# Where weights stand within their places: an offset of a few columns in a transformer layer

## The chip, the core and the metric

The kernel runs on one core of one Trainium2 chip. The metric is the device time of one execution in microseconds; lower is better. The core has a matrix engine (TensorE, in the profile PE, with its weight loads as PEld), a vector engine (VectorE, DVE), an activation engine (ScalarE, ACT), GpSimd (POOL) and SyncE (SP), which issues transfers. SBUF is the on-chip memory of 128 partitions from which the engines read; PSUM takes the results of matmuls, here in banks of 512 fp32 columns.

## What is computed

One transformer layer on a sequence of 512 tokens with 1024 features, in fp32:

```python
h = modulate(rmsnorm(x, norm_ffn1), sh1, sc1)
x = x + 0.5 * g1 * swiglu(h, w_ffn1_in, w_ffn1_out)
h = modulate(rmsnorm(x, norm_mix), sh2, sc2)
qa, ka, va, qb, kb, vb, ga, gb = split(h @ w_in)
ya = window_gqa_sink(rope(qa), rope(ka), va, sink) @ w_branch_a
ob = rmsnorm(diff_attention(rope(qb), rope(kb), vb, lam), subln_b) * (1 - lam_init)
yb = ob @ w_branch_b
x = x + g2 * ((sigmoid(ga) * ya + sigmoid(gb) * yb) @ w_out)
h = modulate(rmsnorm(x, norm_ffn2), sh3, sc3)
x = x + 0.5 * g3 * swiglu(h, w_ffn2_in, w_ffn2_out)
```

The feed-forward width is 2816, `shift`, `scale` and gate `g` of each part come from a conditioning vector, and each SwiGLU splits its incoming product into gate and up half.

## The kernel before

Features stand on the 128 partitions and tokens along the columns, so x is eight tiles of 128 x 512. To keep fp32 accuracy every operand of a product is split into a high part of type fp32r and a low part that holds what is left, and a product is three matmuls: high x high, high x low, low x high (`mm3`, lines 168 to 171; `two`, lines 433 to 441, does this for two outputs with a moving operand of 256 columns).

**Weights and their places.** A tile of weights is 128 x 1024 fp32 (512 KB) or, in the outgoing product of the first SwiGLU, 128 x 128 per input chunk. It comes from HBM into one of four `raw` buffers. ScalarE copies it to the high part, VectorE subtracts to get the low part (`split_from`, lines 179 to 181). In `load_main` (line 973) ScalarE writes the negated copy and a transfer of GpSimd's queue adds the weights to it. High and low parts stand in two long tensors, `high` and `low`, of five places of 1024 columns each. `high_low` (line 186) hands the places out in turn, skipping those held by a feed-forward unit:

```python
i = i * 1024 + aside
return tuple(t[:, i : i + n] for t in parts)
```

`aside` is an offset in columns (4 bytes each) within the place. It is 0, `ASIDE` = 16 or `FAR` = 64. The tensors are 16 columns longer than the five places. A full tile with an offset hangs over into the next place by as many columns, and the framework that adds the waits sees this overlap: the tile then also waits for the readers of those columns in the next place. Before the change the offset is

- 0 in the first SwiGLU's first products, in `project` (line 1031: v, k and q of the second attention), in `project_pairs` (line 1048), in `gates` (line 1077) and in `branch` (line 1498);
- 16 in the feed-forward units (`Unit.prepare`, line 477), in the mix (line 1563) and in the last four outgoing tiles of the first SwiGLU;
- 64 in the other outgoing tiles (`Out1.prepare`, line 771; 768 or 512 columns, so nothing hangs over).

Activations stand in tiles of other tensors: h, the attention outputs and the merged branches in `b8` tiles, the transposed probabilities and some sums in `u4` tiles.

**Order of the work around the change.** The first SwiGLU ends with `Out1`. For its last chunk group the outputs m = 4 to 7 are formed by halves of the tokens in `boundary` (line 355), so that the norm of the first half can run while the second is multiplied: all four m for tokens 0 to 255 (matmuls of 256 columns), then all four again for 256 to 511. Then come the first three gates, by halves, with weights in `u4`, and the projections of v, k and q, where h is the stationary operand and the weights of 512 columns move. `main` (line 1513) goes on with gates 3 and 4 (`EARLY_A` = 5 is where they stop), then `project_pairs` for k and v and for q of the window attention: there, too, h is stationary, and 256 columns of weights move, 48 matmuls a tile, six tiles. The differential attention's scores, transposes and products are put between those matmuls by `Line`, which keeps a list of due pieces at build time. The other gates (5 to 15) are filler while attention runs; their weights are loaded by `load_main` as the stationary operand, with 512 columns of h moving.

Then `branch` multiplies the differential attention's output with w_branch_b for all 512 tokens, beside the window attention, and after that the window attention's output with w_branch_a by halves of the tokens: for each half four tiles of weights, 24 matmuls of 256 columns each. The results, times the gate, are summed in `then_b` (line 1538) by VectorE, which frees one of three `acc` banks, and are split for the mix. The mix multiplies with w_out, eight tiles: six for all tokens (24 matmuls of 512 columns each), the last two by halves (`LAST` = 2) for the norm of the second SwiGLU. The second SwiGLU then runs units with offset 16.

TensorE's order is fixed by the program in these stages; ScalarE, VectorE and the queues of SP and POOL are ordered by the framework's scheduler at build time, outside the parts marked as a manual schedule.

Of the kernel before, what the change touches and what calls it, by code (L numbers as in the profile page):

```python
# [18 lines left out]
P = 128  # L19
D = 1024  # L20
T = 512
NC = D // P
# [77 lines left out]
ASIDE = 16  # L100

FAR = 64

CHUNKS = (range(0, 6), range(6, 12), range(12, 16), range(16, 22))
PLAIN, LAST_1 = 3, 4
# [10 lines left out]
EARLY_A, FETCH = 5, 4.0  # L116
# [13 lines left out]
def layer(ctx: ExitStack, tc: tile.TileContext, a: dict):  # L130
# [10 lines left out]
    def sbuf(tag, shape, dt, bufs):  # L141
        return sb.tile(shape, dt, name=name(tag), tag=tag, bufs=bufs)
# [4 lines left out]
    def f2():  # L147
        return sbuf("f2", [P, T], F32, F2)

    def b8(dt=F32R):  # L150
        return sbuf("b8", [P, 4, T], dt, 12)

    def u4(dt=F32R):
        return sbuf("u4", [P, 2, T], dt, 6)
# [24 lines left out]
    def split_from(hi, lo, src):  # L179
        S.copy(hi, src)  # L180
        V.tensor_tensor(lo, src, f(hi), ALU.subtract)  # L181
# [4 lines left out]
    def high_low(n=1024, aside=0, holder=None):  # L186
        while turn[0] % HILO in holders:
            turn[0] += 1
        i = turn[0] % HILO
        turn[0] += 1  # L190
        if holder:
            holders[i] = holder
        i = i * 1024 + aside
        return tuple(t[:, i : i + n] for t in parts)
# [5 lines left out]
    def load_split(src, n=1024, spare=False, aside=0):  # L200
        raw = sbuf("raw", [P, 1024], F32, RAW)
        if spare:
            hi, lo = (u4().rearrange("p a b -> p (a b)") for _ in range(2))
        else:
            hi, lo = high_low(aside=aside)
        nc.sync.dma_start(raw[:, 0:n], src)
        split_from(hi[:, 0:n], lo[:, 0:n], raw[:, 0:n])
        return hi, lo

    HALVES = (slice(0, 2 * P), slice(2 * P, T))  # L210
    FULL = (slice(0, T),)
# [231 lines left out]
    class Unit:  # L443
# [33 lines left out]
        def prepare(self, q):  # L477

            if q in self.ready:
                return  # L480
            self.ask(q)
            n = self.depth * 2 * P
            if q in self.apart:
                both = b8().rearrange("p a b -> p (a b)")
                hi, lo = both[:, 0:n], both[:, 1024 : 1024 + n]
            else:
                hi, lo = high_low(n, ASIDE, (self, q))
            t = self.at[q]
            with tc.issue_after(copied[0]) if q in self.in_order and copied else nullcontext():
                split_from(hi, lo, t)  # L490
            self.ready[q] = hi, lo
            if q in self.more:
                s, src = self.more[q]
                G.dma_start(t, self.srcs[src], accum_op=ALU.add)
                self.at[s] = t
# [105 lines left out]
    with tc.manual_schedule(engines=BOUND | {mybir.EngineType.SP, mybir.EngineType.Pool}):  # L601
# [60 lines left out]
        for k in range(NC):  # L662
# [17 lines left out]
            wh, wl = w1.pop(k)[3:]  # L680
# [72 lines left out]
    class Out1:  # L753
# [17 lines left out]
        def prepare(self, m):  # L771
            if m not in self.ready:
                self.ask(m)
                t = self.ready[m] = high_low(self.depth * P, ASIDE if self.by_halves(m) else FAR, (self, m))
                with tc.issue_after(copied[0]):
                    split_from(*t, self.at[m])

# [51 lines left out]
    with tc.manual_schedule(engines={mybir.EngineType.SP, mybir.EngineType.Pool}):  # L829
# [4 lines left out]
        for q in range(3, 2 * PLAIN):  # L834

            w = loaded1 or [load_split(a["w1i"][q - 3, k], aside=ASIDE * (q == 5)) for k in range(2)]
            loaded1 = None
            out = pair_banks()
            for k in range(NC):
                wh, wl = w[k // 4]  # L840
                for i in range(2):
                    o = (k % 4) * 256 + i * P
# [11 lines left out]
        for n, chunks in enumerate(CHUNKS):  # L854
# [3 lines left out]
            for p in range(begun, max(chunks.stop // 2, PLAIN + 1)):  # L858
                u, nxt = units1[p], units1.get(p + 1)
# [73 lines left out]
    for i in range(2):  # L933
        o = ROW_LAM + 2 * i * HD
# [35 lines left out]

    hh, hl = new_h()

    def load_main(src):

        raw = sbuf("raw", [P, 1024], F32, RAW)
        nc.sync.dma_start(raw, src)
        hi, lo = high_low()
        S.copy(hi, raw)
        S.activation(lo, raw, AF.Identity, scale=-1.0)
        G.dma_start(lo, src, accum_op=ALU.add)  # L980
        return hi, lo
# [66 lines left out]
    def project_pairs(srcs, then):  # L1048

        n = 2 * P  # L1050
        out = [bank("acc") for _ in range(2)]
        for u, src in enumerate(srcs):
            wh, wl = load_main(src)
            for t in range(NT):
                ht = slice(t * P, (t + 1) * P)
                po = out[t // 2][:, t % 2 * n : (t % 2 + 1) * n]
                for i in range(4):
                    k = 4 * u + i
                    w = slice(i * n, (i + 1) * n)
                    first, last = k == 0 and t % 2 == 0, k == NC - 1 and t % 2 == 1  # L1060
                    PE.matmul(po, hh[k][:, ht], wh[:, w], start=first, stop=False, skip_group_check=True)
                    PE.matmul(po, hh[k][:, ht], wl[:, w], start=False, stop=False, skip_group_check=True)
                    PE.matmul(po, hl[k][:, ht], wh[:, w], start=False, stop=last, skip_group_check=True)
                    yield MM3 / 2
        then(out)
# [11 lines left out]
    def gates(more=lambda: True):  # L1077
        while gate_next[0] < 16 and more():
            j = gate_next[0]
            gate_next[0] += 1  # L1080
            wh, wl = load_main(a["w_gate"][j])
            out = bank("acc")
            for k in range(NC):
                o = k * P
                mm3(out, wh[:, o : o + P], wl[:, o : o + P], hh[k], hl[k], k == 0, k == NC - 1)
                yield MM3
            gate_end(j, out)
# [202 lines left out]
    wa = {}  # L1290
# [204 lines left out]
            turns["w"] = (b, g * nk + kc + 1)  # L1495


    def branch(w, j0, o_h, o_l, then, load, r=FULL[0]):
        for u in range(4):
            with tc.issue_after(banded_last[0]):  # L1500
                wh, wl = load(w[u])
            for i in range(2):
                j = 2 * u + i
                g = f2()[:, r]
                nc.sync.dma_start(g, gate_scr[j0 + j][:, r])
                y = bank("acc")[:, r]
                for k in range(4):
                    o = k * 256 + i * P
                    mm3(y, wh[:, o : o + P], wl[:, o : o + P], o_h[:, k, r], o_l[:, k, r], k == 0, k == 3)
                    yield MM3 * (r.stop - r.start) / T  # L1510
                then(j, g, y, r)

    def main():
        yield from beside(project(vb_w, T, values_b), LATER)
        yield from beside(project(a["w_kb"], T, keys_b), LATER)
        yield from beside(project(a["w_qb"], T, queries_b), LATER)
        yield from beside(gates(lambda: gate_next[0] < EARLY_A), 1)
        while later or asked:
            column(later)
        tables_a()  # L1520
        yield from project_pairs([a["w_kva"][u] for u in range(2)], keys_a)
        for g in range(2):
            yield from project_pairs([a["w_qa"][2 * g + u] for u in range(2)], lambda ps, g=g: queries_a(ps, g))
        yield from gates(lambda: done["b"] < NT)
        line.drain(lambda: done["b"] == NT)
        start_a()
        yield from gates()
        ma = [b8(F32) for _ in range(2)]

        def then_a(j, g, y, r):  # L1530
            V.scalar_tensor_tensor(ma[j // 4][:, j % 4, r], g, 1.0, y, ALU.add, ALU.mult)
            line.helped(0.6)

        yield from branch(a["w_yb"], 8, ob_h, ob_l, then_a, load_main)
        mix.extend(new_h())
        mh, ml = mix

        def then_b(j, g, y, r):
            V.scalar_tensor_tensor(g, g, 1.0, y, ALU.add, ALU.mult)
            m = ma[j // 4][:, j % 4, r]  # L1540
            V.tensor_tensor(m, m, g, ALU.add)
            split_from(mh[j][:, r], ml[j][:, r], m)
            line.helped(1.0)

        for i, r in enumerate(HALVES):
            line.drain(lambda: done["a"] >= 2 * i + 2)
            yield from branch(a["w_ya"], 0, *wa["o"], then_b, load_split, r)

    mix = []
    line.run(main())  # L1550
# [9 lines left out]
    nc.sync.dma_start(cact[0], c_scr.partition_broadcast(P))  # L1560
    mod_begin(G3)
    for m in range(NC):
        w = load_split(a["w_mix"][m], aside=ASIDE)

        def products(po, r, w=w):
            wh, wl = w
            for k in range(NC):
                o = k * P
                mm3(po, wh[:, o : o + P], wl[:, o : o + P], mh[k][:, r], ml[k][:, r], k == 0, k == NC - 1)
                yield  # L1570

        if m >= NC - LAST:
            last.append((m, products))
            continue
        y = bank("sc")
        list(products(y, FULL[0]))
        V.scalar_tensor_tensor(x[m], y, modv[G2][:, m : m + 1], x[m], ALU.mult, ALU.add)
        n3.add(m)
        for _ in range(BESIDE_MIX[m]):
            if latest or asked:  # L1580
                column(latest)
# [242 lines left out]
    u = units[2]  # L1824
# [19 lines left out]
    for v, p in seq:  # L1844
# [7 lines left out]
        u = v  # L1852
# [77 lines left out]
```

## Time and profile before

| | |
|---|---|
| time, median of 3 runs | 1067.63 us (1066.71 to 1070.24) |
| profiled execution | 1065.94 us, its span 1064.2 us |
| matmul records | 7316 |
| moved by DMA | 220.92 MB, mean 208 GB/s |

The profile is one execution as the hardware profiler recorded it. Windows give the busy time of each engine in a stretch of the span. Groups gather equal instructions of a line: the number behind x is the count, then total busy time and the mean in ns of one, then the idle time before them. A name such as `sc<-b,high` says that a PSUM bank sc is written from an activation in b and a weight in high. A matmul's record runs from its start to its modelled end, so records of neighbours overlap.

### The profile page before, as it was taken

The numbers are of one execution on the slowest core, as the hardware profiler recorded it, in microseconds if no ns is written. First come the engines' busy times: TensorE is split into PE (matmuls) and PEld (weight loads), VectorE is DVE, ScalarE is ACT, GpSimd is POOL, SyncE is SP. The second block draws the span as 40 slices with busy tenths as digits, with TensorE's granted clock in tenths as the row PEclk, the third lists the DMA queues.
The fourth block names the chain that finished last, engine by engine and source line by source line (L and its number), as shares of the span: only waits on it lengthen the run. The fifth ranks groups of instructions, "written<-read, shape, count | busy, mean of one in ns | idle before, by whom it ended". The sixth has DMA issues, their size and how long they took to land.

```text
span 1064.2 us, 18654 instructions
## 1 busy us (share of the span) xinstructions
PE 1048.2 (99%) x7316; PEld 955.1 (90%) x7316; DVE 795.8 (75%) x1459; ACT 567.3 (53%) x928; POOL 154.0 (14%) x174
## 2 busy tenths in 40 slices
PE   8999999999999999999999999999999999999998
PEld 6789889899998988898778878989999999999998
DVE  7985667567796679858863587976888787877867
ACT  5564335334354432666775756534766646654553
POOL 1100010100110100443211100001111211112210
PEclk8999999999999999999999999999999999999999
DMA  9968686966885369696357843974498998989974
GB/s 342 365 205 198 210 216 186 281 174 191 257 203 173 120 238 410 208 257 164 82 126 182 232 144 100 358 234 109 101 231 191 227 229 216 220 217 220 213 149 124
DMA packets 69083, 220.92 MB, mean 208 GB/s; under 512 B 8193, under 2 KB 10881, under 8 KB 68994
## 3 DMA queue, kind: packets, MB, share of 16 engines
q1 hardware_dynamic: 46512, 146.52, 38.5%
q0 software_dynamic: 19488, 68.70, 34.7%
q10 hardware_dynamic: 2994, 4.51, 1.2%
q8 instruction: 57, 0.93, 0.4%
q14 instruction: 32, 0.26, 0.1%
HBM read 209.46 MB, written 10.23 MB: 206 GB/s over the span
## 4 chain that ended last, share of the span: by engine, by line
PE 81%; DVE 8%; issue 5%; ACT 3%; DMA 2%; POOL 1%; SPq 0%; DVEq 0%; POOLq 0%; ACTq 0%
PE acc L439 6%; PE acc L441 6%; PE acc L440 6%; PE sc L439 5%; PE sc L440 5%; PE sc L441 5%; PE sc L169 5%; PE sc L170 5%; PE sc L171 5%; PE acc L169 4%; PE acc L170 4%; PE acc L171 4%; PE sc L177 2%; PE acc L1042 2%; PE acc L1043 2%
## 5 line engine op out<-in xcount | busy, mean ns | idle before, releaser
L180 ACT CAST high<-raw 128x1024 fp32r<-128x1024 f32 (+2 forms) x162 | 158.3, 986 | 168.3 <-PE sc L170 41.7
L181 DVE TENSOR_TENSOR low<-raw,high 128x1024 fp32r<-128x1024 f32 (+2 forms) x162 | 183.7, 1142 | 50.7 <-ACT high L180 46.2
L439 PE MATMUL acc<-b,high 128*128 128x256 f32 x508 | 141.0, 278 | 0.3 <-DVE f L518 0.3
L440 PE MATMUL acc<-b,high 128*128 128x256 f32 x508 | 140.6, 277 | 0.1
L441 PE MATMUL acc<-b,low 128*128 128x256 f32 x508 | 140.6, 277 | 0.0
L439 PE MATMUL sc<-b,high 128*128 128x256 f32 x500 | 138.5, 277 | 0.0
L441 PE MATMUL sc<-b,low 128*128 128x256 f32 x500 | 138.5, 277 | 0.1
L440 PE MATMUL sc<-b,high 128*128 128x256 f32 x500 | 138.4, 277 | 0.0
L181 DVE TENSOR_TENSOR low<-u,high 128x1024 fp32r<-128x1024 f32 (+1 forms) x73 | 87.5, 1200 | 30.4 <-ACT high L180 28.9
L180 ACT CAST high<-u 128x1024 fp32r<-128x1024 f32 (+1 forms) x73 | 75.5, 1036 | 58.4 <-PE sc L170 16.9
L169 PE MATMUL sc<-b,high 128*128 128x512 f32 (+1 forms) x280 | 101.0, 361 | 0.0
L170 PE MATMUL sc<-b,high 128*128 128x512 f32 (+1 forms) x280 | 100.7, 360 | 0.0
L171 PE MATMUL sc<-b,low 128*128 128x512 f32 (+1 forms) x280 | 100.6, 359 | 0.0
L439 PEld LDWEIGHTS acc<-b,high 128*128 128x128 f32 x508 | 95.4, 188 | 0.8 <-DVE f L518 0.5
L440 PEld LDWEIGHTS acc<-b,high 128*128 128x128 f32 x508 | 95.5, 188 | 0.4 <-DVE b L1718 0.3
L441 PEld LDWEIGHTS acc<-b,low 128*128 128x128 f32 x508 | 95.4, 188 | 0.0
L439 PEld LDWEIGHTS sc<-b,high 128*128 128x128 f32 x500 | 94.1, 188 | 0.2
L441 PEld LDWEIGHTS sc<-b,low 128*128 128x128 f32 x500 | 93.9, 188 | 0.3 <-DVE low L181 0.3
L440 PEld LDWEIGHTS sc<-b,high 128*128 128x128 f32 x500 | 93.9, 188 | 0.0
L169 PE MATMUL acc<-b,high 128*128 128x512 f32 (+1 forms) x248 | 93.0, 375 | 0.0
L171 PE MATMUL acc<-b,low 128*128 128x512 f32 (+1 forms) x248 | 90.2, 364 | 0.0
L170 PE MATMUL acc<-b,high 128*128 128x512 f32 (+1 forms) x248 | 90.1, 363 | 0.0
(369 smaller groups left out, 2678.1 us busy)
## 6 DMA issues: line engine op xcount, KB each, us to landing
u<-w_mod SPq DMA_DIRECT2D x40, 512.0 KB, 7.7
b<-w_mod SPq DMA_DIRECT2D x32, 512.0 KB, 5.6
raw<-w2i SPq DMA_DIRECT2D x31, 512.0 KB, 5.5
u<-w2i POOLq DMA_DIRECT2D x31, 512.0 KB, 6.7
u<-w1u POOLq DMA_DIRECT2D x24, 512.0 KB, 7.2
raw<-w1u SPq DMA_DIRECT2D x24, 512.0 KB, 6.3
raw<-w1o SPq DMA_DIRECT2D x24, 384.0 KB, 4.2
raw<-w_gate SPq DMA_DIRECT2D x16, 512.0 KB, 6.8
```

The costliest lines, as they stand in the source:

```text
L169: PE.matmul(out, wh, xh, start=first, stop=False)
L170: PE.matmul(out, wh, xl, start=False, stop=False)
L171: PE.matmul(out, wl, xh, start=False, stop=last)
L177: PE.matmul(out, of[j][a], of[j][b], start=i == 0, stop=i == 2)
L180: S.copy(hi, src)
L181: V.tensor_tensor(lo, src, f(hi), ALU.subtract)
L439: PE.matmul(out, wh[:, s], xh, start=first and j == 0, stop=False, skip_group_check=True)
L440: PE.matmul(out, wh[:, s], xl, start=False, stop=False, skip_group_check=True)
L441: PE.matmul(out, wl[:, s], xh, start=False, stop=last and j == 1, skip_group_check=True)
L1042: PE.matmul(out[t][:, 0:n], hh[k][:, ht], wh[:, o : o + n], start=k == 0, stop=False)
L1043: PE.matmul(out[t][:, 0:n], hh[k][:, ht], wl[:, o : o + n], start=False, stop=False)
```

## The change

The offsets within the places are changed for some tiles; no load, no arithmetic and no product is added or taken away.

```diff
+STEP, STEP_1 = 8, 56
+BRANCH_ASIDES = (STEP, ASIDE, ASIDE, ASIDE), (ASIDE, ASIDE, 0, 0)
+MIX_ASIDES = 0, 0, 0, 0, 0, 0, ASIDE, ASIDE
...
-                t = self.ready[m] = high_low(self.depth * P, ASIDE if self.by_halves(m) else FAR, (self, m))
+                aside = FAR if not self.by_halves(m) else STEP_1 if m == NC - LAST_1 else ASIDE
+                t = self.ready[m] = high_low(self.depth * P, aside, (self, m))
...
-    def load_main(src):
+    def load_main(src, aside=0):
...
-        hi, lo = high_low()
+        hi, lo = high_low(aside=aside)
...
-            wh, wl = load_main(src)
+            wh, wl = load_main(src, ASIDE)
...
-            wh, wl = load_main(a["w_gate"][j])
+
+            wh, wl = load_main(a["w_gate"][j], ASIDE * (j == EARLY_A))
...
-    def branch(w, j0, o_h, o_l, then, load, r=FULL[0]):
+    def branch(w, j0, o_h, o_l, then, load, r=FULL[0], asides=(0, 0, 0, 0)):
...
-                wh, wl = load(w[u])
+                wh, wl = load(w[u], aside=asides[u])
...
-            yield from branch(a["w_ya"], 0, *wa["o"], then_b, load_split, r)
+            yield from branch(a["w_ya"], 0, *wa["o"], then_b, load_split, r, BRANCH_ASIDES[i])
...
-        w = load_split(a["w_mix"][m], aside=ASIDE)
+        w = load_split(a["w_mix"][m], aside=MIX_ASIDES[m])
```

In words: the six tiles of the paired projections go from 0 to 16, and the gate tile after them (j = 5) with them. In the second branch (w_branch_a) the first half's tiles go from 0 to 8, 16, 16, 16 and the second half's from 0 to 16, 16, 0, 0. The first of the four halved outgoing tiles (m = 4) goes from 16 to 56. The first six tiles of the mix go from 16 to 0. In the built program the sequence of places is the same as before; the scheduler puts some copies, splits and small vector operations of the attention, second branch and mix in a slightly different order, and TensorE's order differs at two spots of a few matmuls.

## The prediction

> **What bounds the kernel now.** I read the page first, then the stages by windows, then the matmuls by shape inside single stretches, and last the chain of waits.
>
> ```profile
> span 1064.2 us, 18654 instructions
> PE 1048.2 (99%) x7316; PEld 955.1 (90%) x7316; DVE 795.8 (75%) x1459; ACT 567.3 (53%) x928; POOL 154.0 (14%) x174
> PEclk8999999999999999999999999999999999999999
> PE 81%; DVE 8%; issue 5%; ACT 3%; DMA 2%; POOL 1%; SPq 0%; DVEq 0%; POOLq 0%; ACTq 0%
> ```
>
> TensorE is busy for 99% of the span at the full granted clock, and the chain runs through it for 81%. A change that adds and removes no instruction can gain only by the time that one matmul takes, or lose by a new wait. The stages that the change touches (columns: stretch, its length, then busy time and instructions of PE, PEld, DVE, ACT, POOL; clock, DMA share, GB/s):
>
> ```profile
> 346.00:357.00 11.00, 11.00 (x96) 10.93 (x94) 6.37 (x16) 3.88 (x7) 0.71 (x2) 1.00 0.56 187
> 461.00:513.00 52.00, 51.98 (x402) 46.80 (x401) 35.46 (x94) 33.91 (x62) 15.57 (x15) 1.00 0.73 175
> 513.00:560.00 47.00, 45.63 (x260) 34.43 (x260) 36.24 (x98) 35.25 (x81) 10.53 (x10) 1.00 0.50 121
> 600.00:664.00 64.00, 63.48 (x390) 51.87 (x389) 47.72 (x151) 38.23 (x93) 3.75 (x6) 1.00 0.49 149
> 664.00:689.00 25.00, 25.00 (x210) 24.95 (x209) 23.88 (x53) 13.47 (x24) 2.13 (x4) 1.00 0.94 346
> 689.00:722.00 33.00, 33.00 (x143) 26.61 (x142) 25.82 (x37) 10.56 (x15) 0.00 (x0) 1.00 0.76 250
> ```
>
> These are the last outgoing products (346), the paired projections (461), attention with gates as filler (513, 600), the second branch (664) and the mix (689). TensorE has no idle time in three of them and 0.02 us in the paired projections, so there a shorter matmul shortens the span; VectorE is at 23.88 of 25.00 us in the second branch, which matters below.
>
> **What a place is worth.** In the built program the tensor high begins at byte 47,424 of a partition, low at 68,160 and the b8 places at 93,248 and steps of 8,192: all leave 64 on division by 256, and the u4 places leave 160. I call d the distance, modulo 256 bytes, from the start of the moving operand to that of the weights. With an offset of 0 or 64 elements d is 0, with 16 elements it is 64, with 16 elements against a moving operand in u4 it is -32. The same shapes in uninterrupted stretches, the duration of one matmul being the last number before the final bar. First d = 0: 512 columns wide in the early outgoing products (window 120:147), the projections (388:430) and a gate (451:453); then 256 wide in the second branch (668.5:688) and the paired projections (462:469):
>
> ```profile
> L169 PE MATMUL sc<-b,high 128*128 128x512 f32 x41 | 15.9, 389 | 0.0
> L1043 PE MATMUL acc<-low,b 128*128 128x512 f32 x47 | 18.3, 389 | 0.0
> L170 PE MATMUL acc<-b,high 128*128 128x512 f32 x3 | 1.2, 389 | 0.0
> L169 PE MATMUL acc<-b,high 128*128 128x256 f32 x55 | 15.6, 283 | 0.0
> L1062 PE MATMUL acc<-low,b 128*128 128x256 f32 x21 | 5.9, 283 | 0.0
> ```
>
> Now d = 64: 512 wide in the mix (690:721), 256 wide in the halved outgoing products (346.5:355.5); and 256 wide in three feed-forward stretches that follow each other: just after 512-wide products (149:151.6), then against an operand in u4 (151.9:154.5, d = -32), then against b8 again (156:159.9):
>
> ```profile
> L170 PE MATMUL sc<-b,high 128*128 128x512 f32 x45 | 17.8, 396 | 0.0
> L169 PE MATMUL sc<-b,high 128*128 128x512 f32 x45 | 17.6, 395 | 0.0
> L169 PE MATMUL sc<-b,high 128*128 128x256 f32 x27 | 7.6, 281 | 0.0
> L439 PE MATMUL acc<-b,high 128*128 128x256 f32 x8 | 2.2, 281 | 0.0
> L439 PE MATMUL sc<-u,high 128*128 128x256 f32 x8 | 2.2, 280 | 0.0
> L439 PE MATMUL acc<-b,high 128*128 128x256 f32 x12 | 3.3, 276 | 0.0
> ```
>
> Matmuls overlap, so the mean is longer than the distance between two starts. That the differences carry over to the pace is shown by equal stretches (the last bracket is the count of matmuls), 512 wide at d = 0 and at d = 64:
>
> ```profile
> 118.00:148.00 30.00, 30.00 (x134) 1.00 0.77 218
> 690.00:720.00 30.00, 30.00 (x131) 1.00 0.75 246
> ```
>
> 131 in place of 134 in 30 us is 5 ns a matmul, to within one count. So for 512 columns d = 64 costs 396 - 389 = 7 ns, and d = 0 is the better place; for 256 columns d = 0 is the worst (283), and d = 64 has two levels, 281 and 276. Which of them holds depends on what ran before: straight after 512-wide products it is 281 and stays so; after a stretch at a half-line distance (280) it is 276 and stays so. The offsets 8 and 56 give distances of 32 and -32 bytes, half-line like that of the u4 stretch.
>
> **The change part by part.** No instruction is added; PE's order differs in two spots of a few matmuls.
> 1. Mix, six of eight tiles from d = 64 to d = 0: 6 x 8 x 3 = 144 matmuls of 512 columns at 6.5 ns (the mean of 395.5 less 389) = 0.94 us gained. VectorE has 25.82 of 33 us there and can follow. The two last tiles keep 16.
> 2. Second branch: 192 matmuls of 256 columns, 24 a tile. The first tile (offset 8, d = 32) goes from 283 to between 283 and 276; I take 280, its mirror image: 0.07 us. Five tiles go from d = 0 to 64: 120 x 7 = 0.84 us if the step sets the low level, 120 x 2 = 0.24 us if not. I take 0.84, since a half-line stretch precedes. The last two tiles stay at d = 0.
> 3. Halved outgoing products: the first of four m (36 matmuls, offset 56, d = -32) goes from 281 to 280, 0.04 us (between +0.18 and -0.07 us by 276 and 283). The other 108 go from 281 to 276, 0.54 us, or stay, 0. The norm's small fp32 products cut into this run, so I take 0.40.
> 4. Paired projections: 6 tiles x 48 = 288 matmuls. Here the weights are h and the moving operand is the shifted one, so d = -64, which no stretch shows. By its mirror image: 283 to 276 gives 2.02 us, 283 to 281 gives 0.58 us. From below I allow the largest effect of a place with the other sign, 288 x 7 = 2.02 us lost. I take 5 ns, 1.44 us, nearer the low level, because attention's transposes and scores break this run again and again and each break is a chance to fall out of 281.
> 5. The gate after them keeps 16 so that it doesn't overlap its predecessor: 24 matmuls of 512 columns at 6.5 ns = 0.16 us lost.
>
> The shifted tiles hang over into the next place by 16 columns, so such a tile must also wait for the first matmuls that read the tile there, four turns old. That tile is first read right after the own place comes free, and the copies run far ahead of their use:
>
> ```profile
> L980 POOL DMA_DIRECT2D low<-w_qa x4: 862/892/909, 451.9 to 468.8; - x4
> L1061 PE MATMUL acc<-high,b x96: 277/283/386, 461.6 to 512.7; 128*128 128x256 f32 x96
> L206 SPq DMA_DIRECT2D raw<-w_ya x8: 328/330/430, 591.4 to 657.1; - x8
> ```
>
> Two w_kva tiles of 48 matmuls are ahead of the first w_qa tile, whose low part is sent at 451.9 us, while the paired projections only begin at 461.6; a shift of a few microseconds has room. Behind a later copy stand, on ScalarE, the squares of the B queries (L1093), and behind these, through VectorE, their transposes, which are on the chain at 469.72 us:
>
> ```profile
> L1093 ACT ACTIVATE f<-f x8: 623/632/637, 428.2 to 459.5; 128x512 f32<-128x512 f32 x8
> 469.72 0.44 PE tp L1119 x4
> ```
>
> On POOL the powers of these squares stand nearer the front, ahead of the w_qa transfers. The first w_ya tile is asked for at 591.4 us and the branch runs from 664. I cost all of this at nothing; if the cover were gone, one copy and one split would stand in the way, the 1.06 and 1.23 us shown below.
>
> Does the gain of part 4 survive attention? The chain of waits there:
>
> ```profile
> 509.24 0.94 PE sc L177 x6
> 510.17 1.28 DVE sm L1194 x2
> 511.55 1.64 ACT x L1197 x4
> ```
>
> The scores that start VectorE and ScalarE come from TensorE, so an earlier TensorE starts them earlier, and I let the gain pass. From 513 to 560 TensorE already waits 47.00 - 45.63 = 1.37 us; that is where it could be eaten.
>
> Sum: 0.94 + 0.07 + 0.84 + 0.04 + 0.40 + 1.44 - 0.16 = 3.57 us. The profiled execution took 1065.94 us (span 1064.2), so it would take 1062.4; against the median of the runs, 1067.63, it is 1064.1. Single runs spread from 1066.71 to 1070.24, about as much as the effect.
>
> The Trainium skill, in "TensorE: Matmul & The Clock Gate", "Part 2: What happens when you issue a matmul", says that TensorE has two independent SBUF read ports, so that loading the next weights takes nothing from the running matmul. By that rule the place of the weights would be worth nothing and the sum would be 0 us. The rows at one shape, clock and line, 283 against 281 and 276, don't agree with it.
>
> **The rivals.**
> A. The level doesn't switch: 281 stays everywhere. Gain 0.94 + 0.24 + 0.07 + 0.58 - 0.16 = 1.67 us, 1066.0. For it: the halved products ran at 281 for their whole stretch. Against it: 280 is followed by 276. Chance 0.16.
> B. The gain is eaten: part 4 in the waits after 513 us, and part 2 by VectorE, which has only 1.12 us left in the branch. What stays is 3.57 - 1.44 - 0.84 = 1.29 us, 1066.3. Chance 0.09.
> C. Place decides nothing; the levels come from other traffic (DMA share 0.94 in the branch, 0.76 in the mix), and the change does nothing to the time: 1067.6. Against it: the projections run at 389 under heavy DMA and the feed-forward stretches repeat level for level. Chance 0.04. The rule of the Trainium skill on the two read ports, cited above, would come out here.
> D. Slower. VectorE becomes the bound in the second branch. Its order there is changed: splits of the next weights stand ahead of the sums that free the three accumulator banks.
>
> ```profile
> 617.27 1.06 ACT high L180
> 618.36 1.23 DVE low L181
> ```
>
> Each split that gets ahead holds TensorE for up to 1.23 us. Seven run in that stage: 8.6 us, less 3.57, is 5.0 us slower, 1072.7. It decides from three splits on (3.7 us, more than the gain). For it: 23.88 of 25.00 us. Against it: the splits of the mix tiles can slide into the mix, where VectorE is idle for 7 us. Chance 0.10.
>
> **How the numbers follow.** The forecast has 0.61, with its own range of gains from 2.7 us (part 4 at the 281 level) to 4.4 us (all at the low level): 1063.2 to 1064.9. 0.3% is 3.2 us, about what a measurement of this kernel can tell from no change. Of the forecast 0.48 lies beyond it: its middle and its upper end do, only the case of part 4 at 281 doesn't. With 0.04 of A and B by the spread of the runs, faster has 0.52. Of the forecast 0.13, of A, B and C together 0.23 give same 0.36. D, and 0.02 of B and C by the spread, give slower 0.12. The range reaches from 1062.2 (all low, and a microsecond of run spread) to 1068.4 (A to C with the same spread, and the start of D).
>
> **What would show it.** Mix at 389 instead of 396 for 512 columns; the second branch at 276 from its second tile to its sixth and 283 in the last two; the halved products at 276 after the first m; the paired projections below 283; the fifth gate at 396; stage lengths shorter by the parts of the sum. It is wrong if the paired projections run longer than 283, if the branch stays at 281 behind the step, if TensorE's idle time from 513 to 664 us grows by more than a microsecond, or if sums in the branch are released by splits.

## The result, and the profile after

The changed kernel takes 1066.64 us (median of 22 runs, 1064.01 to 1068.90), the kernel before 1068.56 us (median of 22 runs, 1066.71 to 1074.16). The ratio is 0.998, with a 95% interval from 0.9974 to 0.9987: the change saves 1.9 us (1.4 to 2.8), within the 0.3% that the prediction set as the bound of no change, and a little over half of the 3.57 us that its sum promised. The prediction started from the median of three runs, 1067.63 us; from 1068.56 its sum gives 1065.0.

The page of the kernel after, of an execution that took 1068.43 us:

```profile
span 1066.6 us, 18660 instructions
PE 1047.0 (98%) x7316; PEld 953.3 (89%) x7316; DVE 795.7 (75%) x1459; ACT 566.6 (53%) x928; POOL 155.0 (15%) x174
PEclk9999999999999999999999999999999999999999
PE 79%; DVE 8%; issue 5%; DMA 3%; ACT 3%; POOL 1%; SPq 0%; ACTq 0%; DVEq 0%; POOLq 0%
```

The number of matmuls is the same, TensorE is still the bound, and its busy time is 1.2 us less. The span of this one execution is 2.4 us longer than that of before, though the median is shorter. The stages show where the time went. These are the starts of the first matmul of each stage in the timeline (start, duration, then the instruction): halved outgoing products, first gates, projections, paired projections, fifth gate, second branch, mix, halves of the mix. First before, then after, where the lines of the code stand 5 to 7 further down:

```profile
346.29 0.28 PE L169 MATMUL sc<-b,high 128*128 128x256 f32 x1
...
364.58 0.28 PE L169 MATMUL acc<-b,u 128*128 128x256 f32 x1
...
383.91 0.51 PE L1042 MATMUL acc<-high,b 128*128 128x512 f32 x1
...
461.64 0.28 PE L1061 MATMUL acc<-high,b 128*128 128x256 f32 x1
...
513.06 0.40 PE L169 MATMUL acc<-b,high 128*128 128x512 f32 x1
...
663.35 0.28 PE L169 MATMUL acc<-b,high 128*128 128x256 f32 x1
...
688.67 0.40 PE L169 MATMUL sc<-b,high 128*128 128x512 f32 x1
...
722.28 0.28 PE L169 MATMUL sc<-b,high 128*128 128x256 f32 x1
```

```profile
350.51 0.28 PE L174 MATMUL sc<-b,high 128*128 128x256 f32 x1
...
368.56 0.28 PE L174 MATMUL acc<-b,u 128*128 128x256 f32 x1
...
387.73 0.50 PE L1048 MATMUL acc<-high,b 128*128 128x512 f32 x1
...
465.50 0.28 PE L1067 MATMUL acc<-high,b 128*128 128x256 f32 x1
...
516.26 0.40 PE L174 MATMUL acc<-b,high 128*128 128x512 f32 x1
...
666.89 0.28 PE L174 MATMUL acc<-b,high 128*128 128x256 f32 x1
...
691.42 0.40 PE L174 MATMUL sc<-b,high 128*128 128x512 f32 x1
...
724.26 0.28 PE L174 MATMUL sc<-b,high 128*128 128x256 f32 x1
```

The execution of after is 4.22 us late (350.51 - 346.29) before the first tile that the change touches; from there to the end of the span it takes 716.1 us against 717.9, which is 1.8 us less and agrees with the medians. So stages are compared by the distances of such rows, not by the spans. The row of the fifth gate and attention starts at the gate that gets the offset 16 and ends at the branch. A profiled repetition of the changed kernel (below) is the third column of times; gains are against before.

| stage | before | after | repetition | gain, after | gain, repetition | forecast |
|---|---|---|---|---|---|---|
| halved outgoing products | 18.29 | 18.05 | 18.09 | 0.24 | 0.20 | 0.44 |
| first three gates | 19.33 | 19.17 | 19.47 | 0.16 | -0.14 | 0 |
| paired projections | 51.42 | 50.76 | 50.78 | 0.66 | 0.64 | 1.44 |
| fifth gate and attention | 150.29 | 150.63 | 150.72 | -0.34 | -0.43 | -0.16 |
| second branch | 25.32 | 24.53 | 24.52 | 0.79 | 0.80 | 0.91 |
| mix, first six tiles | 33.61 | 32.84 | 32.67 | 0.77 | 0.94 | 0.94 |
| sum | | | | 2.28 | 2.01 | 3.57 |

The largest gap by far stands in the paired projections. The matmuls of after by shape, inside single stretches (last number before the final bar: mean ns of one): in the halved products the first pass behind the tile with offset 56 (352.9:358.5) and the second pass (362.6:368.4), the paired projections (465.5:473.1), the branch behind its first tile (669.8:683), its last two tiles (686:691.2), the mix (692:723):

```profile
L176 PE MATMUL sc<-b,low 128*128 128x256 f32 x16 | 4.5, 281 | 0.0
L175 PE MATMUL sc<-b,high 128*128 128x256 f32 x17 | 4.7, 276 | 0.0
L1068 PE MATMUL acc<-low,b 128*128 128x256 f32 x22 | 6.1, 279 | 0.0
L174 PE MATMUL acc<-b,high 128*128 128x256 f32 x36 | 9.9, 276 | 0.0
L176 PE MATMUL acc<-b,low 128*128 128x256 f32 x15 | 4.2, 283 | 0.0
L174 PE MATMUL sc<-b,high 128*128 128x512 f32 x46 | 17.9, 389 | 0.0
```

The 276 level appears in the branch, and in the halved products only in their second pass. What the levels are worth in pace: in 13 us of the branch, before (669:682), after (672.5:685.5), and in an experiment that stays at 281 (E2, 672:685), the bracket behind the third number holds the count of matmuls:

```profile
669.00:682.00 13.00, 13.00 (x111) 13.00 (x110) 12.76 (x30) 8.12 (x14) 0.00 (x0) 1.00 1.02 388
```

```profile
672.50:685.50 13.00, 13.00 (x117) 13.00 (x116) 13.00 (x33) 8.46 (x15) 0.00 (x0) 1.00 1.02 384
```

```profile
672.00:685.00 13.00, 13.00 (x113) 13.00 (x112) 12.80 (x29) 8.30 (x14) 0.00 (x0) 1.00 1.03 394
```

A window counts every matmul that reaches into it, so the pace is (13,000 + duration of one) / count: 119.7, 113.5 and 117.5 ns. The starts in the traces give it more finely, and these figures are used from here on: 120.0 ns for the rows at 283, 117.8 for those at 281, 113.3 for those at 276; for 512 columns 226.8 at 389 and 233.4 at 396. The paired projections run at 117.8 in spite of their 279: 66 matmuls without a break start between 465.50 (shown above) and this row, 7.66 us / 65:

```profile
473.16 0.28 PE L1069 MATMUL acc<-high,b 128*128 128x256 f32 x1
```

They stand at the level of 281, not of 276. In the attention behind them TensorE's busy time is nearly the same; windows of 150 us before and after, PE's busy time being the second number:

```profile
513.00:663.00 150.00, 147.48 (x855) 117.44 (x855) 99.34 (x303) 98.03 (x229) 20.96 (x23) 1.00 0.56 150
```

```profile
516.00:666.00 150.00, 147.47 (x855) 117.23 (x854) 99.60 (x303) 98.27 (x229) 20.94 (x23) 1.00 0.54 147
```

TensorE idles for 2.52 and 2.53 us. The equal sum hides two changes that the starts show, matmul by matmul. The fifth gate's 24 matmuls take 0.10 us longer, and the next wait of TensorE for VectorE gives it back, first before, then after (the bracket has the idle time):

```profile
529.38 0.63 PE L1119 MATMUL tp<-ident,x 128*128 128x128 f32 x4 [0.89 <-DVE u L181]
```

```profile
532.59 0.63 PE L1126 MATMUL tp<-ident,x 128*128 128x128 f32 x4 [0.80 <-DVE u L186]
```

And late in the stage four transposes come 123.72 us after its start instead of 123.47. They write the one PSUM bank called tp, which must first be read by VectorE's split of the transposes before them, and that split has moved behind other work of VectorE, first before, then after:

```profile
634.18 0.66 DVE L181 TENSOR_TENSOR u<-tp,u 128x512 fp32r<-128x512 f32 x1
...
636.53 0.66 PE L1119 MATMUL tp<-ident,x 128*128 128x128 f32 x4
```

```profile
639.15 0.68 DVE L186 TENSOR_TENSOR u<-tp,u 128x512 fp32r<-128x512 f32 x1
...
639.98 0.63 PE L1126 MATMUL tp<-ident,x 128*128 128x128 f32 x4
```

Before, the split was over 1.69 us ahead of the transposes; after, it ends 0.15 us ahead of them. E8 below shows what this goes with.

### The profile page after: what moved, and what is told of

It reads as the page before. It is cut to its first block, busy times and chain, and to the rows that moved or that the text cites. A ratio compares the mean times of both kernels' runs of the same rounds, so it can differ in the third digit from the quotient of the medians.

```text
span 1066.6 us, 18660 instructions
## 1 busy us (share of the span) xinstructions
PE 1047.0 (98%) x7316; PEld 953.3 (89%) x7316; DVE 795.7 (75%) x1459; ACT 566.6 (53%) x928; POOL 155.0 (15%) x174
## 4 chain that ended last, share of the span: by engine, by line
PE 79%; DVE 8%; issue 5%; DMA 3%; ACT 3%; POOL 1%; SPq 0%; ACTq 0%; DVEq 0%; POOLq 0%
PE acc L444 5%; PE acc L446 5%; PE acc L445 5%; PE sc L174 5%; PE sc L175 5%; PE sc L176 5%; PE sc L446 5%; PE sc L444 5%; PE sc L445 5%; PE acc L174 4%; PE acc L176 4%; PE acc L175 4%; PE sc L182 2%; PE acc L1048 2%; PE acc L1049 2%
```

## The experiments

Each edit is against the changed kernel. A kernel seen once has one profiled execution; since single executions of one kernel differ by more than the effects (before ran from 1066.71 to 1074.16), these are read by stage, with the distances of starts worked out as in the table above. Between after and its repetition four of the six rows above agree within 0.1 us; the mix differs by 0.17 us and the first three gates by 0.30. The single executions of E2 to E9 took 1066.6 to 1068.9 us, too close together to be ranked.

**E1. Does the place decide at all?** All offsets are zero, so d = 0 everywhere except against u4.

```diff
-ASIDE = 16
+ASIDE = 0
-FAR = 64
+FAR = 0
-STEP, STEP_1 = 8, 56
+STEP, STEP_1 = 0, 0
-        parts.append(keep([P, HILO * 1024 + ASIDE], nm, F32R))
+        parts.append(keep([P, HILO * 1024 + 16], nm, F32R))
```

> All offsets 0, the lengths of the two weight tensors kept, so that every 256-wide matmul with a weight in them against a b8 operand stands at d = 0. Theory (place sets the pace): the feed-forward units show 283 in place of 276, some 3,000 matmuls longer by 7 ns, about 20 us in all: near 1087 us; 512-wide stays at 389. Rival (other traffic sets the levels): the units stay at 276 and the time within 2 us of 1066.6.

Measured: 1093.07 us, span 1091.3. The groups of the feed-forward products on the page, first of after, then of E1:

```profile
L444 PE MATMUL acc<-b,high 128*128 128x256 f32 x508 | 141.0, 278 | 0.3 <-DVE f L523 0.3
```

```profile
L444 PE MATMUL acc<-b,high 128*128 128x256 f32 x508 | 144.1, 284 | 0.0
```

The same instructions, at a mean granted clock of 0.998 against 1.000, take 6 ns more at d = 0, and the span is 24.7 us longer, more than the 20 us expected. The branch (25.33 us) and the paired projections (51.40) are back at their times of before, while the mix, whose tiles stand at 0 in both, needs 32.67 as in the repetition. Rival C falls: place decides. The rule of the Trainium skill cited in the prediction ("TensorE: Matmul & The Clock Gate", "Part 2: What happens when you issue a matmul"), two independent read ports, isn't contradicted as such, but it says nothing of the place, and by it alone these two spans would be equal.

**E2. Is it the step that sets the branch's low level?** The first tile of the branch gets 16 like its followers.

```diff
-STEP, STEP_1 = 8, 56
+STEP, STEP_1 = 16, 56
```

> The second branch's first tile at 16 like the next four, without the half-line step of 8. Theory (the step sets the low level): the run of 120 matmuls shows 281 in place of 276, 0.5 us more in the branch. Rival (the attention pieces in front of it set the level): 276 stays, branch within 0.1 us.

Measured: the branch takes 25.04 us, 0.51 more than after. Its matmuls behind the first tile (671.2:685.3):

```profile
L174 PE MATMUL acc<-b,high 128*128 128x256 f32 x41 | 11.5, 281 | 0.0
```

All 123 stand at 117.8 ns. With one tile of 24 matmuls shifted by 32 bytes instead of 64, the 120 behind it run at 113.3. The step does it; the products of the attention that stand among the first tile's matmuls don't. E2 also loses 0.66 us at the start of the mix (33.33 us against 32.67 in the repetition): there TensorE waits for the last splits of the branch's sums on VectorE and ScalarE, which come later in this kernel. The scheduler put the work of these two engines in another order than in after.

**E3. Why does the first pass of the halved products stay at 281?** The offset 56 gives d = -32. If the sign is to blame, 8 (d = 32) must mend it.

```diff
-STEP, STEP_1 = 8, 56
+STEP, STEP_1 = 8, 8
```

> The first halved outgoing tile at offset 8 (d = +32) in place of 56 (d = -32). Theory (the sign of the half-line step decides after 512-wide products): the 54 matmuls of the first pass show 276 in place of 281, 0.24 us less. Rival (no step holds straight after 512-wide products, only one behind a break): 281 stays in the first pass and 276 in the second.

Measured: the stage takes 18.10 us, no less than with 56. First pass behind the step (352.6:358.6), then the second pass (361.9:364):

```profile
L174 PE MATMUL sc<-b,high 128*128 128x256 f32 x18 | 5.1, 281 | 0.0
```

```profile
L174 PE MATMUL sc<-b,high 128*128 128x256 f32 x7 | 1.9, 276 | 0.0
```

The same picture: 54 matmuls at 117.8 ns, and the low level only in the second pass. It isn't the sign alone. What both have in common is that the step tile stands right behind 512-wide products at d = 0.

**E6 and E7. The step one tile later.** The second of the four outgoing tiles gets the step, the first keeps 16, so that 256-wide products stand ahead of the step; with 8 in E6 and 56 in E7. E6 also puts the paired projections and the fifth gate back to 0; E7 gives the mix the offsets 8, 16, 16, 0, 0, 0, 16, 16.

```diff
-aside = FAR if not self.by_halves(m) else STEP_1 if m == NC - LAST_1 else ASIDE
+aside = FAR if not self.by_halves(m) else STEP if m == NC - LAST_1 + 1 else ASIDE
...
-            wh, wl = load_main(src, ASIDE)
+            wh, wl = load_main(src)
...
-            wh, wl = load_main(a["w_gate"][j], ASIDE * (j == EARLY_A))
+            wh, wl = load_main(a["w_gate"][j])
```

> Halved outgoing products: first m at 16, second at 8, the others at 16. If a step works only behind 256-wide products and not straight behind 512-wide ones, the third and fourth m of the first pass show 276 (36 matmuls, 0.16 us). If it needs a break they stay at 281. Besides, the paired projections and gate 5 are back at 0: the projections 283 and 0.6 us longer, attention 0.2 to 0.4 us shorter.

```diff
-aside = FAR if not self.by_halves(m) else STEP_1 if m == NC - LAST_1 else ASIDE
+aside = FAR if not self.by_halves(m) else STEP_1 if m == NC - LAST_1 + 1 else ASIDE
...
-MIX_ASIDES = 0, 0, 0, 0, 0, 0, ASIDE, ASIDE
+MIX_ASIDES = STEP, ASIDE, ASIDE, 0, 0, 0, ASIDE, ASIDE
```

> As before for the outgoing products but the second m at 56 (d = -32): same two outcomes; if the sign matters only one of the two runs shows 276. The mix's eight tiles at 8, 16, 16, 0, 0, 0, 16, 16: if 512-wide matmuls at d = 64 have a low level behind a half-line step, the second and third tile show 389; if not, 396.

Measured: the first pass behind the step in E6 (353.5:358.5), and in E7 (352.8:357.8):

```profile
L174 PE MATMUL sc<-b,high 128*128 128x256 f32 x16 | 4.4, 276 | 0.0
```

```profile
L174 PE MATMUL sc<-b,high 128*128 128x256 f32 x15 | 4.1, 276 | 0.0
```

Now 46 (E6) and 45 (E7) of the 48 matmuls between the step and the norm's first small products run at the low pace, and the stage takes 17.95 and 17.93 us, 0.1 less than with the step in front. Either sign works; what decided here is what stands ahead of the step: eighteen 256-wide matmuls at d = 64 in place of 512-wide ones at d = 0. Width and distance weren't taken apart. E6's paired projections need 51.41 us, the time of before, which prices the change's part 4 once more: 0.65 us. In E7 the mix's first three tiles, one at d = 32 and two at 64 (695.2:706):

```profile
L174 PE MATMUL sc<-b,high 128*128 128x512 f32 x16 | 6.3, 396 | 0.0
```

512-wide products have no low level behind a step: 232.8 ns at d = 32, 233.3 at 64 right behind it, 227.1 at 0.

**E4. Is there a low level at d = -64?** The first tile of the paired projections gets 8 (here d = -32), and the seventh mix tile too. This kernel's output is wrong, by a relative error of 0.058, and the cause wasn't found; its matmuls are the same in number and shape, and only their times are used.

```diff
-MIX_ASIDES = 0, 0, 0, 0, 0, 0, ASIDE, ASIDE
+MIX_ASIDES = 0, 0, 0, 0, 0, 0, STEP, ASIDE
...
-    def project_pairs(srcs, then):
+    def project_pairs(srcs, then, first=ASIDE):
-            wh, wl = load_main(src, ASIDE)
+            wh, wl = load_main(src, ASIDE if u else first)
...
-        yield from project_pairs([a["w_kva"][u] for u in range(2)], keys_a)
+        yield from project_pairs([a["w_kva"][u] for u in range(2)], keys_a, STEP)
```

> A step of 8 in two more places: the first tile of the paired projections and the seventh tile of the mix (first of the halved two). Theory A (a step sets the low level wherever it stands): mix halves and the first units of the second SwiGLU go from 281 to 276, about 0.8 us less; paired projections go to 276 only until attention's first break. Theory B (d = -64 has no low level): paired projections stay at 281 behind the step. If a step needs a break or another sign the mix halves stay at 281.

Measured: the second tile right behind the step (469.9:471.5), and behind the first four transposes (472.3:474):

```profile
L1068 PE MATMUL acc<-low,b 128*128 128x256 f32 x5 | 1.4, 276 | 0.0
```

```profile
L1068 PE MATMUL acc<-low,b 128*128 128x256 f32 x5 | 1.4, 279 | 0.0
```

The low level exists at d = -64: 17 matmuls at 113.7 ns. This step tile, too, stands right behind 512-wide products, those of the third and fourth gate, and yet it worked; it has 48 matmuls in place of 18, and the weights are the moving operand. Which of the two makes the difference wasn't tried. The first four transposes end it, and what comes behind them runs at 117.8, as in the changed kernel. The stage takes 50.65 us, 0.11 less. In this stage a break by transposes doesn't offer a chance to fall to the low level, it takes the low level away. The halves of the mix gain nothing: the step stands right behind 512-wide products there, the tile behind it stays at 117.8 ns, and the step tile also came late. TensorE idled 0.97 us for its high part, which is in the mix's 33.79 us, and 0.80 us for its low part, so that the halves took 13.83 us instead of 12.64.

**E5. Which distance gives which pace?** Every tile of the branch gets another offset: 8, 2, 4, 6 and 16, 16, 12, 14 columns. The mix has 16 in its first three tiles.

```diff
-BRANCH_ASIDES = (STEP, ASIDE, ASIDE, ASIDE), (ASIDE, ASIDE, 0, 0)
-MIX_ASIDES = 0, 0, 0, 0, 0, 0, ASIDE, ASIDE
+BRANCH_ASIDES = (STEP, 2, 4, 6), (ASIDE, ASIDE, 12, 14)
+MIX_ASIDES = ASIDE, ASIDE, ASIDE, 0, 0, 0, ASIDE, ASIDE
```

> The second branch's eight tiles at 8, 2, 4, 6 and 16, 16, 12, 14 columns (d = 32, 8, 16, 24, 64, 64, 48, 56 bytes), the mix's eight at 16, 16, 16, 0, 0, 0, 16, 16. If one distance has the low level by itself, some tile of 24 matmuls shows 276 whatever stands before it. If a 64-byte line is the unit and only the fall from a half-line step sets it, the tiles between 0 and 64 lie between 283 and 276 and only the two at 16 can be at 276. Mix: 396 in the first three tiles, 389 in the next three, 0.47 us more than with six at 0.

Measured, tile by tile from the second on: d = 8 (670.1:672.5), 16 (672.9:675.4), 24 (675.8:678.3), 64 (679:683.8), 56 (687:689.3); then the mix at d = 64 (690:706.4) and at 0 (707:722.8):

```profile
L174 PE MATMUL acc<-b,high 128*128 128x256 f32 x8 | 2.2, 277 | 0.0
...
L174 PE MATMUL acc<-b,high 128*128 128x256 f32 x8 | 2.2, 281 | 0.0
...
L174 PE MATMUL acc<-b,high 128*128 128x256 f32 x8 | 2.3, 285 | 0.0
...
L174 PE MATMUL acc<-b,high 128*128 128x256 f32 x15 | 4.1, 276 | 0.0
...
L174 PE MATMUL acc<-b,high 128*128 128x256 f32 x7 | 2.0, 280 | 0.0
...
L174 PE MATMUL sc<-b,high 128*128 128x512 f32 x24 | 9.5, 395 | 0.0
...
L174 PE MATMUL sc<-b,high 128*128 128x512 f32 x24 | 9.3, 389 | 0.0
```

In paces (mean distance of starts): 115.5 ns at d = 8, 118.5 at 16, 121.5 at 24, 113.3 at 64 from the fourth matmul on, 117.9 at 48, 117.6 at 56. So d = 64 in its low level is the fastest place found for 256 columns, d = 24 the slowest, and the tile at d = 24, which follows tiles at 8 and 16, serves as a step too, so a step need not be 32 bytes. Each distance was seen in one tile behind one neighbour, so this map mixes the distance with what stands ahead. The mix gives part 1 again inside one execution: 72 matmuls at 233.3, 72 at 226.8 ns.

**E8. What does the shifted branch cost elsewhere?** All tiles of the branch at 0; everything else as changed.

```diff
-BRANCH_ASIDES = (STEP, ASIDE, ASIDE, ASIDE), (ASIDE, ASIDE, 0, 0)
+BRANCH_ASIDES = (0, 0, 0, 0), (0, 0, 0, 0)
```

> The second branch's offsets back at 0, the rest of the change kept. Theory: the branch takes 25.3 us again (283 throughout), 0.8 us more, and the attention in front of it, which grew by 0.3 us with the change, falls back to about 150.5 us, since the later copies of shifted tiles stood in its way. Rival (the extra 0.3 us comes from elsewhere): attention stays at 150.8 to 151.0.

Measured: the branch takes 25.33 us, as before, and the attention ahead of it 150.42, against 150.63 and 150.72 in the two executions of the changed kernel and 150.29 before. The starts tell where it comes from. In all ten traces with a shifted branch the split of tp stands late, as shown in the section before, and from there to the branch TensorE falls back by 0.24 to 0.29 us against before: 0.15 at these transposes, the rest later. In E8, and in E1 where the branch is at 0 as well, the split stands where it stood before, and nothing is lost behind it. So about 0.24 us of attention go with the branch's offsets: 0.15 through the order in which the scheduler puts VectorE's work at these transposes, the rest not followed up. E8's remaining 0.13 us arise ahead of that point, where the twelve later traces scatter between 0.05 and 0.20; they aren't the fifth gate's, which TensorE has made good 16 us after that gate's start.

**E9. Another distance for the paired projections.** Offset 2 for these six tiles and the fifth gate, d = -8 and 8; their low parts come from VectorE here, and the step of the outgoing products is the later one of E6.

```diff
-            wh, wl = load_main(src, ASIDE)
+            wh, wl = load_split(src, aside=2)
...
-            wh, wl = load_main(a["w_gate"][j], ASIDE * (j == EARLY_A))
+            wh, wl = load_split(a["w_gate"][j], aside=2) if j == EARLY_A else load_main(a["w_gate"][j])
```

> The paired projections' tiles and gate 5 at 2 columns (d = -8 and 8 bytes), their low parts formed by VectorE instead of the accumulating transfer; outgoing step on the second m. The offset map showed 115.5 ns from start to start at d = 8 behind a step. If that pace belongs to the distance, the paired projections show about 278 to 279 through attention's breaks as well, 0.6 us less than at 281; if it came from the step before it, they stay at 281 to 283.

Measured: the paired projections take 50.94 us, between those at -64 (50.76) and at 0 (51.42); their first 66 matmuls run at 120.1 ns, later ones at 117 to 120. d = -8 has no low level of its own here. The 115.5 ns at +8 (E5) stood behind a step and with the weights stationary, so whether the sign, the step or the role of the operand makes the difference isn't shown.

**E10 and E11. Two more steps, and the change again.** E10 adds to the change the later step of E6 and a step in the first unit behind the mix, tile a11. E11 is the changed kernel itself, on the same chip; E10 ran 8 times and E11 11 times.

```diff
+        in_order, offsets = (), {}
...
-                hi, lo = high_low(n, ASIDE, (self, q))
+                hi, lo = high_low(n, self.offsets.get(q, ASIDE), (self, q))
...
+    plain.offsets = {"a11": STEP}
```

> The change with the step on the second halved outgoing tile and a step of 8 on the second SwiGLU's first tile. Theory (a step behind 256-wide products at d = 64 sets the low level): the first units after the mix go from 281 to 276, 0.3 to 0.6 us less there, 0.1 us less in the outgoing products; ratio to the kernel before 0.9975 to 0.998. Rival (breaks and waits in that stage set the level back): unchanged there.

> The changed kernel once more on the same chip, to stand beside the one with two more steps: 0.998 of the kernel before, as measured.

Measured: E10 1066.72 us (ratio to before 0.9969, interval 0.9956 to 0.9983), E11 1066.65 us (0.9975, 0.9964 to 0.9985); before on that chip 1069.26. The intervals overlap, so E10 isn't shown to be better. Its trace says why it can't be by much. The first pass of its halved products has 46 of 48 matmuls at 113.4 ns as in E6, but small products of the norm took 0.15 us longer in this execution, and the stage 18.11. And the stage behind the mix takes 43.63 us against 43.67 and 43.75 in the two executions of the change. Behind the step only nine matmuls in a row reach the low pace there, and small products of the norm end it; the later ones (737:780) stand at the upper level, E10 first, then after:

```profile
L446 PE MATMUL sc<-b,low 128*128 128x256 f32 x46 | 12.9, 280 | 0.0
```

```profile
L446 PE MATMUL sc<-b,low 128*128 128x256 f32 x46 | 12.9, 281 | 0.0
```

So the expected gain of 0.3 to 0.6 us behind the mix didn't come. E11 confirms the change: 2.6 us less than before there, 1.6 to 3.8 by its interval.

After and E11 are one kernel, and yet twelve of their products in this stage stand at different levels, with the same work ahead of them on TensorE (after 751.5:752.9, then E11 750.05:751.5):

```profile
L444 PE MATMUL acc<-b,high 128*128 128x256 f32 x4 | 1.1, 277 | 0.0
```

```profile
L444 PE MATMUL acc<-b,high 128*128 128x256 f32 x4 | 1.1, 281 | 0.0
```

These stand behind waits. So TensorE's order alone doesn't fix the level there.

## Why the prediction was wrong, and where it was right

- **Place decides, and by how much** (the levels 283, 281, 276 and 389, 396): right. E1 and E5 show it within one execution and between two.
- **Part 1, the mix**, 144 matmuls at 6.5 ns, 0.94 us: right. The tiles stand at 389 and 226.8 ns; the repetition, E6 and E8 have 32.67 to 32.69 us, a gain of 0.92 to 0.94. The profiled execution of after has 0.77. There the first tile's last products wait for VectorE: its last split of a sum ends 4.99 us behind the mix's first matmul, in the repetition 4.70, and TensorE gets there at 5.01.
- **Part 2, the branch**, 0.91 us: right, 0.79 measured. In starts the level is worth 120 x (120.0 - 113.3) = 0.80 us, a little less than the 7 ns of the durations gave. The step sets the low level, all 120 matmuls take it (E2 without it loses 0.51), the last two tiles stay at 283. Rival D stood on VectorE, which is indeed busy for 13.00 of 13.00 us in the window shown; TensorE is too, and no wait grew inside the branch. D's mechanism, a split of VectorE that holds TensorE, does show at its real size elsewhere: 0.15 us at the transposes in attention, and at the start of the mix about 0.15 us in after, nothing in the repetition and 0.66 us in E2.
- **Part 3, the halved products**, 0.44 us: half right, 0.24 and 0.20 measured. The step that failed is that the tile at offset 56 lowers the three m behind it. (The prediction calls 32 bytes half a line; no run here shows a line of 64 bytes.) With the weights as the stationary operand it doesn't behind 512-wide products (E3, and the same in E4's mix); one tile later it does, with either sign (E6, E7). The second pass reaches the low level behind its own step tile in all of these kernels.
- **Part 4, the paired projections**, 1.44 us: this is the step that failed, and it holds 0.78 of the 1.29 us that are missing. The prediction took 5 ns a matmul, "nearer the low level, because attention's transposes and scores break this run again and again and each break is a chance to fall out of 281". The stage runs at 117.8 ns from end to end: 288 x (120.0 - 117.8) = 0.63 us, measured 0.66. E4 shows that the low level exists at that distance and that the breaks of this stage work the other way: the first four transposes end it. The prediction's case of 283 to 281 was 0.58, and that is what it should have taken; the evidence it had, that a level lasts until something sets another, gave no reason for a break to set the lower one. The loss that it allowed for the other sign of d didn't come.
- **Part 5, the fifth gate**, -0.16: the gate is 0.10 us longer, and the cost doesn't last, since TensorE waits that much less for VectorE 16 us after the gate's start (0.80 in place of 0.89 us). The prediction charged it to the whole.
- **Attention**, put at nothing apart from this gate: 0.34 and 0.43 us lost. The prediction looked for the cost of the shifted tiles in late copies, and for a changed order of VectorE's work only in the branch. About 0.24 us go with the branch's offsets (E8, E1), 0.15 of them through that order at four transposes of the attention; the rest lies ahead of it, where the traces scatter.
- The first three gates moved by 0.16 and -0.14 us in two executions of one kernel. Their products, too, have two levels, 117.4 and 120 ns in these traces, and the change doesn't touch their offsets. So this is scatter, not gain.
- **Rivals.** A gave 1.67 us and came nearest to the measured 1.9, but not for its reason: the level does switch, in the branch, where A said that it doesn't. B's loss of parts 4 and 2 is refuted by the stages, which gain 0.66 and 0.79 us while TensorE's idle time in attention stays at 2.53 us; C by E1; D by the branch's 24.53 us.

The gaps by row, forecast less gain of after: part 4 0.78, part 3 0.20, attention 0.18, mix 0.17, branch 0.12, less 0.16 of the gates, together 1.29 us: 3.57 - 2.28.

## What to carry to other kernels

Where TensorE is busy all the time with operands in SBUF, the relative place of the two operands within 256 bytes is a parameter to be measured: here all offsets at zero cost 24.7 us more than those chosen, at equal instructions. It must be measured by shape (the best place for 512 columns was 0 and for 256 columns 64) and inside the real sequence, because what stands ahead of a run can decide its pace, and because an offset can change the order that the scheduler gives to other engines (0.15 us at one place here). When a state with two levels is seen, ask for each neighbour which level it sets before a level is put into a sum; and compare single executions by the distances of starts of stages, not by spans.

## What the runs showed of the hardware that wasn't expected

- At d = 64 the pace of 256-wide products depends on what ran before, for as long as nothing intervenes. 117.8 ns held behind 512-wide products and, in the paired projections, behind transposes, 113.3 behind a tile at d = 32, -32 or 24 that itself stands behind 256-wide products, and in E4 behind one at -32 that stands behind 512-wide products. In the branch the step tile starts behind 512-wide products, and transposes and 256-wide products of attention stand among its matmuls. The low level held through 120 matmuls in the branch, and 17 in E4 until transposes came. Behind waits it also differs between two executions of one kernel (113.6 and 117.8 ns in after and E11), so there is something else that these runs don't show.
- A step tile of 18 or 24 matmuls right behind 512-wide products ran at the same 117 to 118 ns as elsewhere, but left the upper level behind it (E3, the mix of E4), while one of 48 with the weights moving left the lower one (E4). Why isn't shown.
- No such memory showed in the 512-wide products of the mix: 226.8 ns at d = 0, 232.8 at 32, 233.3 at 64, the last both behind a step and without one (E5, E7).
- The pace wasn't smooth in d in the one sequence tried (E5): 121.5 ns at 24 stood between 118.5 at 16 and 117 to 118 at 32.
